# FFN weights split one unit ahead, a fourth seven-product pair, two low halves by accumulating transfer, and the position table moved to layer 0

## The chip, the cores and the metric

The kernel runs on one core of one Trainium2 chip. The metric is the device time of one execution in microseconds. Three runs of the kernel before gave a median of 2230.79 us (2229.18 to 2231.19).

## What is computed

A two-layer encoder trunk on 256 frames of width 2048, in float32. Layer 0 mixes the frames by retention and a gated window unit, layer 1 by a gated linear recurrence and a sparse attention with a relative position bias; after either mixer stands a SwiGLU feed-forward network (FFN) of inner width 5632. Cut to what matters here:

```python
def swiglu(h, wg, wu, wd):
    return (jax.nn.silu(h @ wg) * (h @ wu)) @ wd

for layer in range(2):
    h = rms_norm(x, ln_mix_g[layer])
    x = x + (even_mixer(h, ...) if layer == 0 else odd_mixer(h, ..., rel_bias))
    h = rms_norm(x, ln_ffn_g[layer])
    x = x + swiglu(h, w_ffn_gate[layer], w_ffn_up[layer], w_ffn_down[layer])

# in odd_mixer, the relative bias of the attention's logits
bias = rel_bias[rel_bucket(idx - t[None, :, None])]
```

## The kernel before, in words

Every weight is read from HBM once, as float32, and multiplied in three products of 128x512 tiles: weight and activation are each cut into a high part that TensorE takes exactly (`hi`) and a rest (`lo`), and high times high, high times low and low times high are accumulated in PSUM.

**Loading and splitting.** `load` (L92) brings one 1 MB tile, called a unit here, into one of three `raw` buffers over SP's queue. `piece` (L99) splits half a unit: ACT copies it into `hi` (L103), DVE subtracts into `lo` (L104); there are four `hi` and four `lo` buffers, so two units are split at most. A `raw` buffer is free again when its last reader on ACT or DVE is done, and SP, which issues in order, then starts the third load after it.

**Gate and up.** `gate_up` (L282) makes 512 columns of both gate and up. It is called eleven times in each layer, in parts of four, four and three; behind each part come the `down` products of that part (four column blocks, `gemm`, L125). A call takes eight units, each a pair of 128-row slices of gate and up, which hold a 2x2 block of weights. Five units go by eight products each, of three matmuls, so 24 matmuls. Three units, `MIXED = (1, 4, 6)` (L31), go by a Winograd form of seven products, so 21 matmuls: it needs four sums of the weight blocks (`sum`, L317 to L319, on DVE), and splits three weight blocks (`hu`, `lu`) and the four sums (`ht`, `lt`; L324, L325). `sum`, `hu`, `lu`, `ht` and `lt` have one buffer each. The products collect in eight PSUM banks, `q1` to `q8`, of which 1, 5, 6, 7 belong to the four banks of tag `sm`, and 2, 3, 4, 8 to the four of tag `mm`.

**End of a group.** When the last seven-product unit is done, ACT copies `q1` and DVE makes `u2`, `u3`, `v`, `w` (L338 to L343); when the eighth unit is done DVE adds the other banks (L350), and ACT and DVE do the gate (L353, L354). The result is put on a list, `late`, and transposed by PE into two `sm` banks (`pt_hid`, L188) when the next call has done its first unit; ACT and DVE split the transposes into `hid` (L194, L195).

**Order.** The program is written unit by unit: load, split, multiply. A scheduler lays the instructions of each engine in one queue, and each engine takes its queue in order.

**The position table.** Before layer 1's mixer, POOL loads `onehot` and `rel_bias`, PE multiplies them (`pbias`, L555), ACT copies the result to `bt` (L557), and POOL writes it 128 times into a table in HBM (`skew`, 1536 KB, L558), from which layer 1 reads its bias (L843). The first matmuls of layer 1's mixer, `pz` (L581), of 360 columns, read eight units `od_z` of 720 KB.

Of the kernel before, what the change touches and what calls it, by code (L numbers as in the profile page):

```python
# [10 lines left out]
F32 = mybir.dt.float32  # L11
# [3 lines left out]
OP = mybir.AluOpType  # L15
# [11 lines left out]
RAW = 3  # L27
WARM = 7
TB = 17
TF = 10  # L30
MIXED = (1, 4, 6)  # L31
# [5 lines left out]
def trunk(ctx: ExitStack, tc: tile.TileContext, d: dict, out: bass.AP):  # L37
# [4 lines left out]
    wp = ctx.enter_context(tc.tile_pool(name="weights", bufs=4))  # L42
# [56 lines left out]
    def piece(raw, o, k, n):  # L99
        e = k * n  # L100
        hi = wp.tile([128, 1024], F32R, tag="hi", name="hi")
        lo = wp.tile([128, 1024], F32R, tag="lo", name="lo")
        nc.scalar.copy(hi[:, :e], raw[:, o : o + e])  # L103
        nc.vector.tensor_sub(lo[:, :e], raw[:, o : o + e], hi[:, :e].bitcast(F32))  # L104
        return (hi[:, :e].rearrange("p (k n) -> p k n", n=n), lo[:, :e].rearrange("p (k n) -> p k n", n=n))

# [175 lines left out]
    def gate_up(w, n, fp):  # L282
# [3 lines left out]
        q = {}  # L286

        def bank(i):
            if i not in q:
                q[i] = (PS if i in (1, 5, 6, 7) else PM)([512], f"q{i}")  # L290
                return q[i], True
            return q[i], False

        def product(i, x2, hi, lo, last=False):
            (xh, xl), (ps, first) = x2, bank(i)
# [4 lines left out]
        c = {}  # L300
        for j in range(8):
            raw = load(w[j], 2048)
            end = j == 7
            if j not in MIXED:
                a = n.tiles[j]
                for o, cols in ((0, ((2, 0), (4, 1))), (1024, ((3, 0), (8, 1)))):
                    hi, lo = piece(raw, o, 2, 512)
                    for i, th in cols:
                        t = slice(128 * th, 128 * th + 128)
                        for e in range(2):  # L310
                            kt = 1 - e if o else e
                            product(i, (a[:, kt, 0, t], a[:, kt, 1, t]), hi[:, e, :], lo[:, e, :], end and e == 1)
            else:
                a11, a12, a22, d1, d2, d3, d4 = n.tiles[j]
                r = raw.rearrange("p (i n) -> p i n", i=4)
                sm = fp.tile([128, 4, 512], F32, tag="sum", name="sum")
                nc.vector.tensor_add(sm[:, 0:2, :], r[:, 0:3:2, :], r[:, 3:4, :].to_broadcast([128, 2, 512]))  # L317
                nc.vector.tensor_add(sm[:, 2, :], sm[:, 0, :], r[:, 2, :])
                nc.vector.tensor_add(sm[:, 3, :], sm[:, 2, :], r[:, 1, :])  # L319
                parts = []  # L320
                for src, m, name in ((r[:, 0:3, :], 3, "u"), (sm, 4, "t")):
                    hi = fp.tile([128, m, 512], F32R, tag="h" + name, name="h" + name)
                    lo = fp.tile([128, m, 512], F32R, tag="l" + name, name="l" + name)
                    nc.scalar.copy(hi, src)  # L324
                    nc.vector.tensor_sub(lo, src, hi.bitcast(F32))  # L325
                    parts += [(hi[:, i, :], lo[:, i, :]) for i in range(m)]
                b11, b21, b22, s1, s2, s3, s4 = parts
                last = j == MIXED[-1]
                product(1, a11, *b11, last)
                product(2, a12, *b21)  # L330
                product(3, d3, *b22)
                product(5, d1, *s1, last)
                product(7, d4, *s2, last)
                product(6, d2, *s3, last)
                product(4, a22, *s4)
                if last:
                    c1 = T([512], "c1")
                    nc.scalar.copy(c1, q[1])  # L338
# [652 lines left out]
```

## Time and profile before

| | |
|---|---|
| median of three runs | 2230.79 us (2229.18 to 2231.19) |
| profiled execution: its own time | 2230.81 us |
| profiled execution: span | 2229.0 us |
| busy PE, DVE, ACT, POOL | 2211.7, 1613.1, 1107.1, 12.1 us |
| weights read from HBM | 414.29 MB, 188 GB/s over the span |
| FFN of layer 0, FFN of layer 1 (from the transposes) | about 387 to 1097, 1518 to 2225 us |

The profile is one execution seen by the hardware profiler. A matmul's length in it is the time through the array and overlaps the next one's; how fast PE goes is read from the distance between starts. PE's share of busy time is therefore no measure of its pace.

### The profile page before, as it was taken

What the parts mean: (1) busy time and instruction counts of PE and PEld (TensorE: products, weight loads), DVE (VectorE), ACT (ScalarE), POOL (GpSimd) and SP (SyncE); (2) the same over time, 40 slices, a digit from 0 to 9 for tenths busy, and PEclk for the clock granted to TensorE, in tenths of its full rate; (3) what the DMA queues carried; (4) which work ended last, traced back from release to release, by engine and by line L of the source; (5) the groups of instructions that cost most, each with busy time, mean ns of one, the idle gap of its engine ahead of it and who ended that gap; (6) DMA issues with size and microseconds to landing.
All of it is one profiled execution on the core that took longest, in us unless ns stands there. A gap on an engine that the chain in (4) does not pass through costs nothing.

```text
span 2229.0 us, 26164 instructions
## 1 busy us (share of the span) xinstructions
PE 2211.7 (99%) x10199; PEld 1833.3 (82%) x10199; DVE 1613.1 (72%) x2161; ACT 1107.1 (50%) x1302; POOL 12.1 (1%) x24
## 2 busy tenths in 40 slices
PE   9999999999999999999989999999999999999999
PEld 7888888888888888888878888888888888888887
DVE  6745667988578965886535788869885688857974
ACT  6444436655445543554445355546554455434543
POOL 0000000000000000000000000000000000000000
PEclk9999999999999999999999999999999999999999
DMA  8555444554565455555555343355554555456544
GB/s 328 203 192 190 156 167 177 219 208 170 189 217 203 184 186 192 208 205 183 152 192 198 128 154 130 120 188 208 200 200 168 213 198 195 182 192 225 190 170 151
DMA packets 63435, 419.65 MB, mean 188 GB/s; under 512 B 7672, under 2 KB 7672, under 8 KB 15696
## 3 DMA queue, kind: packets, MB, share of 16 engines
q1 hardware_dynamic: 60704, 412.51, 51.0%
q0 software_dynamic: 1312, 3.33, 0.8%
q10 hardware_dynamic: 1296, 2.15, 0.3%
q8 instruction: 80, 1.31, 0.2%
q14 instruction: 43, 0.35, 0.0%
HBM read 414.29 MB, written 3.67 MB: 188 GB/s over the span
## 4 chain that ended last, share of the span: by engine, by line
PE 97%; DMA 1%; DVE 1%; ACT 0%; issue 0%; SPq 0%; ACTq 0%
PE q L296 14%; PE q L297 14%; PE q L298 14%; PE pd L149 7%; PE pd L148 7%; PE pd L147 7%; PE po L149 3%; PE po L148 2%; PE po L147 2%; PE pqk L149 1%; PE pqk L148 1%; PE pqk L147 1%; PE plv L758 1%; DMA raw<-in_od_z 1%; PE pt_hid L188 1%; PE pvs L147 1%
## 5 line engine op out<-in xcount | busy, mean ns | idle before, releaser
L103 ACT CAST hi<-raw 128x1024 fp32r<-128x1024 f32 (+3 forms) x652 | 677.6, 1040 | 936.1 <-PE q L298 277.4
L104 DVE TENSOR_TENSOR lo<-raw,hi 128x1024 fp32r<-128x1024 f32 (+3 forms) x652 | 781.8, 1206 | 492.1 <-ACT hi L103 490.6
L297 PE MATMUL q<-lo,A 128*128 128x512 f32 x880 | 343.1, 390 | 0.0
L296 PE MATMUL q<-hi,A 128*128 128x512 f32 x880 | 343.1, 390 | 0.0
L298 PE MATMUL q<-hi,A 128*128 128x512 f32 x880 | 342.6, 389 | 0.0
L147 PE MATMUL pd<-hi,hid 128*128 128x512 f32 x704 | 274.7, 390 | 0.0
L149 PE MATMUL pd<-hi,hid 128*128 128x512 f32 x704 | 274.0, 389 | 0.0
L148 PE MATMUL pd<-lo,hid 128*128 128x512 f32 x704 | 273.9, 389 | 0.0
L296 PEld LDWEIGHTS q<-hi,A 128*128 128x128 f32 x880 | 165.2, 188 | 35.3
L297 PEld LDWEIGHTS q<-lo,A 128*128 128x128 f32 x880 | 165.2, 188 | 35.3
L298 PEld LDWEIGHTS q<-hi,A 128*128 128x128 f32 x880 | 165.2, 188 | 35.0
L325 DVE TENSOR_TENSOR lt<-sum,ht 128x2048 fp32r<-128x2048 f32 x66 | 151.0, 2287 | 44.9 <-ACT ht L324 44.9
L324 ACT CAST ht<-sum 128x2048 fp32r<-128x2048 f32 x66 | 126.2, 1912 | 59.8 <-PE q L298 51.9
L149 PEld LDWEIGHTS pd<-hi,hid 128*128 128x128 f32 x704 | 132.1, 188 | 27.4
L148 PEld LDWEIGHTS pd<-lo,hid 128*128 128x128 f32 x704 | 132.2, 188 | 27.3
L147 PEld LDWEIGHTS pd<-hi,hid 128*128 128x128 f32 x704 | 132.2, 188 | 27.1
L325 DVE TENSOR_TENSOR lu<-raw,hu 128x1536 fp32r<-128x1536 f32 x66 | 115.7, 1753 | 14.6 <-ACT hu L324 14.6
L324 ACT CAST hu<-raw 128x1536 fp32r<-128x1536 f32 x66 | 97.6, 1479 | 49.6 <-PE q L298 32.9
L297 PE MATMUL q<-lt,A 128*128 128x512 f32 x264 | 104.5, 396 | 0.0
L298 PE MATMUL q<-ht,A 128*128 128x512 f32 x264 | 104.3, 395 | 0.0
L296 PE MATMUL q<-ht,A 128*128 128x512 f32 x264 | 103.6, 395 | 0.0
L317 DVE TENSOR_TENSOR sum<-raw 128x1024 f32<-128x1024 f32 x66 | 80.3, 1217 | 0.0
(385 smaller groups left out, 3411.0 us busy)
## 6 DMA issues: line engine op xcount, KB each, us to landing
raw<-in_wgu SPq DMA_DIRECT2D x176, 1024.0 KB, 4.8
raw<-in_wd SPq DMA_DIRECT2D x88, 1024.0 KB, 4.8
raw<-in_ev_in SPq DMA_DIRECT2D x44, 1024.0 KB, 4.8
raw<-in_od_in SPq DMA_DIRECT2D x32, 1024.0 KB, 4.8
raw<-in_ev_out SPq DMA_DIRECT2D x16, 1024.0 KB, 4.9
raw<-in_od_out SPq DMA_DIRECT2D x16, 1024.0 KB, 4.7
raw<-in_od_z SPq DMA_DIRECT2D x8, 720.0 KB, 4.3
raw<-in_ev_in SPq DMA_DIRECT2D x6, 512.0 KB, 7.2
```

Source lines behind the costliest of these rows:

```text
L103: nc.scalar.copy(hi[:, :e], raw[:, o : o + e])
L104: nc.vector.tensor_sub(lo[:, :e], raw[:, o : o + e], hi[:, :e].bitcast(F32))
L147: mm(ps[th], xh[:, c], hi[:, j, :], start=i + j == 0, stop=False)
L148: mm(ps[th], xh[:, c], lo[:, j, :], start=False, stop=False)
L149: mm(ps[th], xl[:, c], hi[:, j, :], start=False, stop=i + j == total - 1)
L188: nc.tensor.transpose(pt[:, j, 128 * th : 128 * th + 128], srcs[th][:, 128 * j : 128 * j + 128], ident)
L296: mm(ps, xh, hi, start=first, stop=False)
L297: mm(ps, xh, lo, start=False, stop=False)
L298: mm(ps, xl, hi, start=False, stop=last)
L317: nc.vector.tensor_add(sm[:, 0:2, :], r[:, 0:3:2, :], r[:, 3:4, :].to_broadcast([128, 2, 512]))
L324: nc.scalar.copy(hi, src)
L325: nc.vector.tensor_sub(lo, src, hi.bitcast(F32))
```

## The change

Nothing is computed otherwise than in float32 by the same three products, but six things are done differently.

1. `KINDS = "sasrsasr"` names how each of the eight units of a gate/up call is made: `s` by seven products, `r` by eight with both parts made as before, `a` by eight with the low part made by a transfer. There are four `s`, two `a` and two `r` units, where there were three seven-product units and five others.
2. For an `a` unit ACT writes `hi` and, by a second instruction, minus `hi` into `al`; POOL then issues a transfer that reads the same half unit from HBM again (512 KB) and adds it onto `al`. DVE has no part in it. The two halves rotate through three buffers.
3. The four sums of an `s` unit are split in two pieces through the common `hi` and `lo` buffers; its products are taken in the order 5, 7, 6, 4, 1, 2, 3, with the sums first and the plain blocks (`hu`, `lu`) last.
4. The units of a whole FFN, `down` included, form one list. Ahead of the use of unit i the loads and splits of unit i+1 (`s`, `r`) and i+3 (`a`) are written into the program.
5. The transposes of a group's result come behind the next call's eighth unit, not its first. In the first call of a layer the units go in the order `FIRST`.
6. `onehot`, `pbias`, `bt` and the write of `skew` stand in layer 0, ahead of its output projection, not ahead of layer 1's mixer. (`val` of layer 1 moves to a buffer of tag `A`.)

```diff
+HI = 4
+ACC = 3
-MIXED = (1, 4, 6)
+KINDS = "sasrsasr"
+AHEAD = {"s": 1, "r": 1, "a": 3}
+FIRST = (1, 0, 3, 2, 5, 4, 6, 7)
+MIXED = tuple(i for i, c in enumerate(KINDS) if c == "s")
...
+    def piece_acc(raw, src, o, fp):
+        hi = fp.tile([128, 1024], F32R, tag="ah", name="ah", bufs=ACC)
+        lo = fp.tile([128, 1024], F32R, tag="al", name="al", bufs=ACC)
+        nc.scalar.copy(hi, raw[:, o : o + 1024])
+        nc.scalar.activation(lo, hi.bitcast(F32), AF.Copy, scale=-1.0)
+        nc.gpsimd.dma_start(lo, src[:, o : o + 1024], accum_op=OP.add)
...
+    def whole(src, kind, fp):
+        raw = load(src, 2048)
+        out = []
+        for o in (0, 1024):
+            hi, lo = piece_acc(raw, src, o, fp) if kind == "a" else piece(raw, o, 2, 512)
+            out += [(hi[:, i, :], lo[:, i, :]) for i in range(2)]
+        return out
...
+    def sums(src, fp):
+        raw = load(src, 2048)
+        r = raw.rearrange("p (i n) -> p i n", i=4)
+        sm = fp.tile([128, 4, 512], F32, tag="sum", name="sum")
+        nc.vector.tensor_add(sm[:, 0:2, :], r[:, 0:3:2, :], r[:, 3:4, :].to_broadcast([128, 2, 512]))
+        nc.vector.tensor_add(sm[:, 2, :], sm[:, 0, :], r[:, 2, :])
+        nc.vector.tensor_add(sm[:, 3, :], sm[:, 2, :], r[:, 1, :])
+        parts = []
+        for i in range(2):
+            hi, lo = piece(sm.rearrange("p i n -> p (i n)"), 1024 * i, 2, 512)
+            parts += [(hi[:, e, :], lo[:, e, :]) for e in range(2)]
+        hu = fp.tile([128, 3, 512], F32R, tag="hu", name="hu")
+        lu = fp.tile([128, 3, 512], F32R, tag="lu", name="lu")
+        nc.scalar.copy(hu, r[:, 0:3, :])
+        nc.vector.tensor_sub(lu, r[:, 0:3, :], hu.bitcast(F32))
...
-            if j == 0:
-                flush()
+            if i == (0 if self.first else 7):
+                flush()
...
+        units = []
         for g0, gn in ((0, 4), (4, 4), (8, 3)):
             hid = []
             for g in range(g0, g0 + gn):
-                late.append(partial(to_mix2, gate_up(wgu[g], n, fp), "hid", hid))
+                gu = GateUp(n, hid, g == 0)
+                units += [(wgu[g, j], KINDS[j], partial(gu.use, i)) for i, j in enumerate(gu.order)]
             for c in range(4):
-                ps = two(512, "pd")
-                gemm(ps, wd[c], pairs(hid), 512, range(g0, g0 + gn))
...
+                dn = Down(c, hid, gn, done if g0 == 8 else lambda c: None)
+                units += [(wd[c, g0 + i], "r", partial(dn.use, i)) for i in range(gn)]
+        ready = {}
+        for i, (_, _, use) in enumerate(units):
+            for k in range(i, min(i + 4, len(units))):
+                src, kind, _ = units[k]
+                if k not in ready and k - i <= AHEAD[kind]:
+                    ready[k] = sums(src, fp) if kind == "s" else whole(src, kind, fp)
+            use(ready[i])
+            ready[i] = None
...
+    onehot = T([384], "onehot")
+    nc.gpsimd.dma_start(onehot[0:32], d["onehot"])
...
     nc.scalar.copy(bt[0:8], ps[0:8])
     nc.gpsimd.dma_start(skew, bt[0:8, None, :].to_broadcast([8, 128, 384]))
+
+    out_proj(d["ev_out"], ((mixa, (2, 3)), (mixb, (0, 1))), nf0)
```

How the queues change is seen at two places. The first is DVE's queue at the end of a gate/up group. Before, with the lows of the seventh unit (`lu`, then `lt`) around the adds that end the group:

```order
L325 TENSOR_TENSOR lu<-raw,hu 128x1536
L340 TENSOR_TENSOR u_3601<-c_3599,q_3420 128x512
L341 TENSOR_TENSOR u_3602<-u_3601,q_3416 128x512
L342 TENSOR_TENSOR v<-q_3412,u_3601 128x512
L343 TENSOR_TENSOR w<-q_3412,u_3602 128x512
L350 TENSOR_TENSOR c_3599<-q_3340,c_3599 128x512
L350 TENSOR_TENSOR u_3602<-q_3347,u_3602 128x512
L350 TENSOR_TENSOR v<-q_3358,v 128x512
L325 TENSOR_TENSOR lt<-sum,ht 128x2048
```

With the change, between the sixth and the seventh call of a layer; the first two rows still belong to the old call (the eighth unit's `lo`, the seventh unit's `lu`), the sums, their two `lo` and the second `lu` to the next call's first unit:

```order
L109 TENSOR_TENSOR lo<-raw,hi 128x1024 x2
L320 TENSOR_TENSOR lu<-raw,hu 128x1536
L310 TENSOR_TENSOR sum<-raw 128x1024
L311 TENSOR_TENSOR sum<-sum,raw 128x512
L312 TENSOR_TENSOR sum<-sum,raw 128x512
L109 TENSOR_TENSOR lo<-sum,hi 128x1024
L372 TENSOR_TENSOR u_5579<-c_5578,q_5324 128x512
L109 TENSOR_TENSOR lo<-sum,hi 128x1024
L373 TENSOR_TENSOR u_5580<-u_5579,q_5320 128x512
L374 TENSOR_TENSOR v<-q_5316,u_5579 128x512
L375 TENSOR_TENSOR w<-q_5316,u_5580 128x512
L320 TENSOR_TENSOR lu<-raw,hu 128x1536
```

Behind these stand one add of a bank (L381), the two `hid` splits (L218), three more adds, the gate (L384) and the sums of the next call's third unit. So the whole preparation of a seven-product unit now stands ahead of the adds of a group's end.

The second place is ACT's queue in layer 0, where the last retention block ends and the output projection begins. Before:

```order
L103 CAST hi<-raw 128x1024 x8
L483 COPY qkT<-pqkT 128x512 x2
L508 ACTIVATE junk,rss<-pav 128x256 x4
L103 CAST hi<-raw 128x1024 x2
L194 CAST mixb<-pt_mixb 128x2x256
```

With the change:

```order
L108 CAST hi<-raw 128x1024 x8
L607 COPY bt<-pbias 8x384
L549 COPY qkT<-pqkT 128x512 x2
L574 ACTIVATE junk,rss<-pav 128x256 x4
L108 CAST hi<-raw 128x1024 x2
```

`bt` is copied there behind the splits of the projection's first units, and POOL's write of `skew` is issued behind it.

## Rows read from the trace of the kernel before

**Rows 1.** The page, part 1: busy us (share of the span) and instructions.

```profile
PE 2211.7 (99%) x10199; PEld 1833.3 (82%) x10199; DVE 1613.1 (72%) x2161; ACT 1107.1 (50%) x1302; POOL 12.1 (1%) x24
```

**Rows 2.** Engines by stretch: us, busy (count) by engine, PEclk, DMA share, GB/s.

```profile
473.97:516.81 42.84, 42.84 (x193) 35.17 (x192) 38.19 (x38) 23.21 (x21) 0.00 (x0) 1.00 0.54 197
...
560.00:689.00 129.00, 129.00 (x571) 106.47 (x570) 86.19 (x81) 60.01 (x55) 0.00 (x0) 1.00 0.56 202
1097.00:1180.00 83.00, 74.31 (x373) 65.81 (x373) 41.62 (x79) 37.67 (x64) 1.10 (x1) 0.94 0.55 166
```

**Rows 3.** PE's matmuls in order of time, 1117 to 1135 us: start, length.

```profile
1118.14 0.33 PE L148 MATMUL pz<-lo,A 128*128 128x360 f32 x1
1118.31 0.32 PE L149 MATMUL pz<-hi,A 128*128 128x360 f32 x1
1126.56 0.67 PE L147 MATMUL pz<-hi,A 128*128 128x360 f32 x1 [7.92 <-ACT hi L103]
...
1134.98 0.33 PE L149 MATMUL pz<-hi,A 128*128 128x360 f32 x1
```

**Rows 4.** DMA issues, 1098 to 1134 us: engine, count, KB, median us to landing.

```profile
raw<-in_od_z SPq DMA_DIRECT2D x4, 720.0 KB, 22.0
skew<-bt POOLq DMA_DIRECT2D x1, 1536.0 KB, 34.8
```

**Rows 5.** PE's matmuls in order of time: first one of each weight pair.

```profile
485.04 0.39 PE L296 MATMUL q<-hi,A 128*128 128x512 f32 x1
...
490.48 0.40 PE L296 MATMUL q<-hu,A 128*128 128x512 f32 x1
...
495.38 0.39 PE L296 MATMUL q<-hi,A 128*128 128x512 f32 x1
...
500.84 0.40 PE L296 MATMUL q<-hu,A 128*128 128x512 f32 x1
...
505.74 0.39 PE L296 MATMUL q<-hi,A 128*128 128x512 f32 x1
```

**Rows 6.** The chain of waits, 425 to 480 us: the hidden transposes.

```profile
431.12 0.87 PE pt_hid L188 x8
...
473.97 0.87 PE pt_hid L188 x8
```

**Rows 7.** DVE's groups by form, 387 to 517 us: busy us, mean ns.

```profile
L104 DVE TENSOR_TENSOR lo<-raw,hi 128x1024 fp32r<-128x1024 f32 x32 | 38.4, 1216 | 2.3 <-ACT hi L103 2.1
L325 DVE TENSOR_TENSOR lt<-sum,ht 128x2048 fp32r<-128x2048 f32 x10 | 22.8, 2284 | 3.8 <-ACT ht L324 3.8
L325 DVE TENSOR_TENSOR lu<-raw,hu 128x1536 fp32r<-128x1536 f32 x9 | 15.8, 1750 | 1.4 <-ACT hu L324 1.4
L317 DVE TENSOR_TENSOR sum<-raw 128x1024 f32<-128x1024 f32 x9 | 10.9, 1215 | 0.0
...
L195 DVE TENSOR_TENSOR hid<-pt_hid,hid 128x512 fp32r<-128x512 f32 x4 | 2.6, 686 | 0.5 <-ACT hid L194 0.5
...
L340 DVE TENSOR_TENSOR u<-c,q 128x512 f32<-128x512 f32 x3 | 2.0, 679 | 0.0
```

**Rows 8.** ACT's groups by form, 387 to 517 us: busy us, mean ns.

```profile
L103 ACT CAST hi<-raw 128x1024 fp32r<-128x1024 f32 x31 | 32.6, 1053 | 40.3 <-PE q L298 34.4 <-DMA raw<-in_wgu 4.9 <-ACT hi L103 0.8
L324 ACT CAST ht<-sum 128x2048 fp32r<-128x2048 f32 x10 | 19.1, 1912 | 8.5 <-PE q L298 5.7 <-DVE sum L319 2.8
L324 ACT CAST hu<-raw 128x1536 fp32r<-128x1536 f32 x9 | 13.3, 1477 | 5.0 <-PE q L298 3.9 <-ACT hid L194 0.9
```

**Rows 9.** Engines by stretch, matmuls into `po` alone: us, PE, PEld, DVE, PEclk, DMA, GB/s.

```profile
287.00:307.00 20.00, 13.71 (x56) 9.95 (x55) 1.35 (x2) 1.00 0.34 113
```

**Rows 10.** DMA over one gate/up group, 473.97 to 516.81 us: queue's share, landing.

```profile
q1 hardware_dynamic: 1152, 8.39, 53.3%
...
raw<-in_wgu SPq DMA_DIRECT2D x8, 1024.0 KB, 4.8
```

**Rows 11.** DMA issues of the whole span, one further row.

```profile
masks<-in_masks POOLq DMA_DIRECT2D x1, 448.0 KB, 3.3
```

More of the change, by code (lines that the diff above doesn't have):

```diff
@@ L41, in trunk @@
     cpool = ctx.enter_context(tc.tile_pool(name="consts", bufs=1))
-    wp = ctx.enter_context(tc.tile_pool(name="weights", bufs=4))
+    wp = ctx.enter_context(tc.tile_pool(name="weights", bufs=HI))
     act = ctx.enter_context(tc.tile_pool(name="acts", bufs=8))
@@ L280, in out_proj, with __init__, product @@
                     late.append(partial(norm.feed, c))
[L282 to L295, printed above, removed]
+    def sums(src, fp):
[13 more added lines that the diff above has]
+        nc.vector.tensor_sub(lu, r[:, 0:3, :], hu.bitcast(F32))
+        parts += [(hu[:, i, :], lu[:, i, :]) for i in range(3)]
+        return parts
+    class GateUp:
+        def __init__(self, n, hid, first):
+            self.n, self.q, self.hid, self.first = n, {}, hid, first
+            self.order = FIRST if first else range(8)
+        def product(self, i, x2, hi, lo, last=False):
+            first = i not in self.q
+            if first:
+                self.q[i] = (PS if i in (1, 5, 6, 7) else PM)([512], f"q{i}")
+            (xh, xl), ps = x2, self.q[i]
             mm(ps, xh, hi, start=first, stop=False)
@@ L298, in product, with use @@
             mm(ps, xl, hi, start=False, stop=last)
[L300 to L308, printed above, removed]
+        def use(self, i, w):
+            j, end = self.order[i], i == 7
+            if KINDS[j] != "s":
+                a = self.n.tiles[j]
+                for e, kt, cols in ((0, 0, ((2, 0), (4, 1))), (1, 1, ((2, 0), (4, 1))), (3, 0, ((3, 0), (8, 1))), (2, 1, ((3, 0), (8, 1)))):
+                    for b, th in cols:
@@ L361, in ffn, with done @@
         fp = f.enter_context(tc.tile_pool(name=f"sums{layer}", bufs=1))
+        def done(c):
+            if norm is None:
+                for th in range(2):
+                    nc.scalar.dma_start(out[:, th, 512 * c : 512 * c + 512], x[c][:, th, :])
+            else:
+                late.append(partial(norm.feed, c))
+        units = []
         for g0, gn in ((0, 4), (4, 4), (8, 3)):
```

124 lines of the change are left out of this document (63 added, 61 removed).

## The prediction, made before the result was known

> **What bounds the kernel now.** I read the busy times first: PE is busy for 2211.7 of 2229.0 us, DVE for 1613.1 [rows 1]. A busy PE can still be a waiting one, so next come the stretches [rows 2]. In a gate/up group and in the down products PE has no idle time and full clock; in the window around the start of layer 1 it is busy for only 74.31 of 83 us, and the clock was granted at 0.94 of full. That is the one large hole. In the gate/up group DVE is busy for 38.19 of 42.84 us, so it has 4.7 us to spare; in the down products it is busy for two thirds of the time.
>
> The hole: one matmul starts at 1118.31 us and the next at 1126.56, which waited 7.92 us for ACT's `hi` [rows 3]. ACT waited for weights: the four `od_z` loads of that window took 22.0 us from issue to landing while POOL's `skew` write, 34.8 us long, was under way [rows 4]. From 1118.31 to 1134.98 there are 27 steps between matmuls; at 0.17 us (1118.14 to 1118.31) they need 4.6 us, and took 16.67. The hole costs **12.1 us**, of which the matmuls at half pace after the wait (the lower clock of rows 2) are a part.
>
> Elsewhere the pace of PE is the bound, and I take it from starts [rows 5]. An eight-product unit takes 5.44 us (485.04 to 490.48), or 5.46 behind a seven-product one (495.38 to 500.84); a seven-product unit takes 4.90 (490.48 to 495.38, again to 505.74). Three of 4.90, three of 5.46 and two of 5.44, with 0.87 of transposes, make 42.8; the group's measured period is 42.85 (431.12 to 473.97) [rows 6]. So PE does nothing but multiply there.
>
> **The change, part by part.**
>
> *A fourth seven-product unit.* It saves only 0.52 us, not three of 24 matmuls, since these matmuls step more slowly (4.90/21 = 0.233 against 5.44/24 = 0.227) and the next unit begins slower: four of 4.90 and four of 5.46 with 0.87 are 42.31, against 42.83. Twenty-two groups: **-11.4 us**, if nothing waits.
>
> *DVE's and ACT's load.* Before, ten `lo` of 1.216 and three times (1.215 + two of 0.68 + 1.750 + 2.284) are 32.0 us a group; after, four `lo` and four times (1.215 + 2 x 0.68 + 1.750 + 2 x 1.216) are 31.9, the adds of 128x512 priced by `u` [rows 7]. DVE's load stays the same: the accumulating transfer pays for the fourth unit. ACT had ten of 1.053 and three of 1.912 + 1.477, together 20.7; it gets 27.0 with twelve copies of 1.053 for `r` and `a` units (the negation priced as the copy that is nearest to it) and four times 2 x 1.053 + 1.477 [rows 8]. With 23.21 of 42.84 us busy before [rows 2] it becomes 29.5: neither fills its engine.
>
> *The position table.* Its write no longer meets the 720 KB loads, so the hole goes: **-12.1 us**. It now meets the output projection of layer 0. There a unit lasts 5.44 us, as it also has 24 matmuls of 512 columns, and of the 20 us from 287 on 6.3 go to other products than the projection's [rows 9]. So in 34.8 us PE uses (34.8 - 6.3)/5.44 = 5.2 units. In the old place a unit lasts 24 x 0.17 = 4.1 us, so PE wanted 8.5 units in 34.8 us; a wait of 7.92 us means that it had 1.9 too few, 6.6. Four of these were the loads that landed [rows 4], so 2.6 were in stock. Four loads of 720 KB are 2.8 units of 1 MB; 2.6 + 2.8 = 5.4 against 5.2, a margin of a fifth of a unit: **+1 us**, with 0 and the old 12.1 as ends. `pbias` and `bt` keep their cost; `bt` stands behind eight splits that PE has not used up.
>
> *Where the change adds a wait.* Unit i's `raw` buffer serves three loads later. By the program's order of loads (seventh, eighth, next call's second, next call's first) the first unit of a call takes the buffer of the seventh unit of the call before. That one is free when its `lu` is written, and `hu` and `lu` have one buffer, free at the end of the fifth unit. So, from a call's start: fifth unit ends at 3 x 4.90 + 2 x 5.46 = 25.6; `hu` on ACT 1.48 and `lu` on DVE 1.75 [rows 7, 8] give 28.9, or 29.9 where `lu` stands behind both `lo` of the eighth unit, as in the queue shown; the load lands 4.8 us later [rows 10], at 33.7 to 34.7. DVE must then do three sums (2.6), two `lo` (2.4), `u2`, `u3`, `v`, `w` (2.7), `lu` (1.75), one bank's add (0.68) and the first `hid` split (0.69): 10.8 us by lengths, 10.3 as these overlap a little (38.19 us busy where the lengths of rows 7 make 40.3). That is 44.0 to 45.0. The bank it frees is wanted by the third product of the next call, at 42.31 + 6 x 0.233 = 43.7. PE is late by 0.3 to 1.3; I take 0.8. The same delay reaches the third unit's first `lo`, so it is not paid twice. It applies where a call follows a call that itself follows one, with transposes pending, and the queue has this order: three times a layer, six in all, **+4.8 us**. In the other ten boundaries either no transposes are pending or the queue has `lu` earlier; the same walk leaves PE 0.2 to 0.5 us of margin. In the first call of a layer two seven-product units stand side by side and `lu` comes 0.4 us late: +0.8 for both layers, and with it 5.6.
>
> *The accumulating transfers.* There are 88, of 512 KB. No row shows such a transfer. From below, a plain POOL load of 448 KB lands in 3.3 us [rows 11]; from above, `skew` with 34.8 us for 1536 KB gives 11.6 for 512. An `a` unit is prepared three units ahead; by the walk its transfers are issued 10 us or more before PE needs them. I take 5 us, near the load, since both ends of it are whole rows in all 128 partitions, where `skew` is written from 8; so nothing at 5, and at 11.6, since four of them make 46.4 us where a group has 42.3, 4.1 us a group or 90 in all. DMA's share in a group was 53.3% for 8.39 MB [rows 10]; 2.1 MB more make 67%.
>
> The Trainium skill says (DMA: Bandwidth & Descriptors, Rules for kernel authors) that an accumulating transfer reads its destination and writes it later. No run here shows it; by that rule the 2.1 MB count about twice, an estimate of 80% from the same row, which leaves the sum as it is but makes the second rival likelier.
>
> **Sum.** 2230.8 (the profiled execution's own time; the median is the same to 0.1) - 11.4 - 12.1 + 1 + 5.6 = 2213.9; I say **2214**.
>
> **The rivals.**
>
> *No waits at all.* The lengths of rows overstate DVE's work, and a `raw` load could land at 4.7. Then the sum is 2230.8 - 11.4 - 12.1 = 2207. For it: DVE's spare 4.7 us a group. Against: the walk has margins of tenths.
>
> *The transfers slow the weight loads; slower than before.* An `a` unit's transfers for the next call are issued just behind its neighbour's `hu`, at about 31 us, when the load for the next call's first unit is in flight. Eight loads fill 53.3% of 42.84 us, 2.85 us each; a transfer of half the bytes would fill the engines for 1.43 us by its bytes and for 11.6 at `skew`'s pace. I take twice the former, 2.85 us, and if it goes first that load lands 2.85 later. Sixteen boundaries then cost up to 2.85 us more each, less the margin of about 0.4 in ten: 2214 + 41 = 2255. It decides against the change from 17/16, about 1.1 us later landing. For it: the `od_z` loads that took 22.0 us beside a POOL transfer [rows 4]. Against: the transfer starts after the load in the walk, and 33% of the engines' time stays free. The Trainium skill has the rule under which this would happen (same page, Queues, rings and completion order): each DMA engine takes packets from the queues in turn.
>
> *The hole only moves.* `skew` starves the projection as it starved `pz`, 12.1 us again: 2214 - 1 + 12 = 2225. For it: the margin above is a fifth of a unit. Against: each unit there lasts 1.4 times as long.
>
> **How the numbers follow.** A measurement of this kernel tells a difference of about 0.2% (4.5 us) from none. Forecast 0.45 (2214), no waits 0.27 (2207), the transfers 0.19 (2255), the hole moves 0.09 (2225, faster by a little or the same). Faster by over 0.2%: 0.45 + 0.27 and a quarter of 0.09, 0.74; within 0.2%: 0.07; slower: 0.19. The range runs from 2204, under the no-wait sum by what a pace nearer 0.227 would add, to 2246, which takes in the moved hole and half of the third case.
>
> **What would show it.** Right: no PE wait at `pz`; loads of `od_z` back near 4 us; gate/up groups at 42.3 to 43.6 us between transposes; DVE idle for some 4 us a group ahead of the first sum, on DMA `raw`; transfers of `al` landing in about 5 us. Wrong: groups over 44 us, landing of `raw` over 6 us, PE waiting for `al`, or a PE wait in the output projection of layer 0 near 310 to 330 us.

## The result and the profile after

The changed kernel takes 2286.53 us (median of 4, 2284.41 to 2289.23); the kernel before, on the same chip, 2230.89. The ratio is 1.0252, 95% interval 1.0234 to 1.0269: slower by 56 us, where 2214 was forecast.

The page of the kernel after, part 1 (busy us, share of the span, instructions):

```profile
PE 2226.1 (97%) x10133; PEld 1821.6 (80%) x10133; DVE 1615.3 (71%) x2235; ACT 1220.6 (53%) x1482; POOL 88.2 (4%) x112
```

PE is busy 14.4 us longer with 66 fewer matmuls, and DVE about as long as before (1615.3 against 1613.1) [rows 1]. So the busy times do not show where the 56 us are; starts do. The table below goes by PE's starts in the profiled executions: a stage lasts from its first matmul to the first of the next, and an FFN ends with the start of its last matmul.

| stage, us | before | after | change |
|---|---|---|---|
| layer 0 up to its projection | 282.3 | 282.7 | +0.3 |
| projection to FFN | 97.5 | 104.7 | +7.2 |
| FFN of layer 0 | 714.4 | 749.2 | +34.8 |
| between the layers | 1.1 | 0.2 | -0.8 |
| layer 1's mixer, `pz` to FFN | 415.2 | 402.9 | -12.3 |
| FFN of layer 1 | 711.6 | 738.9 | +27.4 |

These add to +56.6, the difference of the two spans (2285.6 and 2229.0). All of what the FFNs lose is in gate/up; the `down` parts are the same within 0.1 us (87.95 before and 88.05 after, for four column blocks of four units). Within gate/up, the first four calls of a layer lose 22.2 and 17.6 us, the next four 10.0 and 7.4, the last three 2.3 and 2.0.

Four stretches of the kernel after (us, then busy us and count of PE, PEld, DVE, ACT, POOL, then PEclk, DMA share, GB/s):

```profile
326.00:331.00 5.00, 1.76 (x5) 0.83 (x4) 1.71 (x2) 2.49 (x3) 0.00 (x0) 0.77 0.51 214
331.00:338.00 7.00, 7.00 (x23) 5.49 (x23) 5.36 (x6) 2.55 (x3) 0.00 (x0) 0.68 0.68 246
486.60:537.90 51.30, 46.59 (x192) 36.41 (x190) 38.68 (x42) 28.36 (x30) 3.48 (x4) 0.93 0.68 209
1139.00:1156.00 17.00, 17.00 (x108) 16.90 (x107) 12.41 (x29) 9.14 (x15) 0.00 (x0) 1.00 0.48 152
```

The first two rows are the projection of layer 0: PE is busy for 1.76 of 5 us, and then its clock is granted at 0.68 of full. That is the hole of [rows 2, 3], smaller, in its new place. The last row is the start of layer 1's mixer, where that hole was: PE busy all 17 us, full clock. The third row is the third call of gate/up in layer 0: 51.3 us, with PE busy 46.59, at a clock of 0.93. DVE is busy for no more than 38.68 of them, ACT 28.36, so no engine bounds this group; and the DMA engines, at 0.68, have room on average.

DMA of the whole span (queue: packets, MB, share of 16 engines; then issues: count, KB each, median us to landing):

```profile
q1 hardware_dynamic: 60704, 412.51, 49.2%
q0 software_dynamic: 13984, 49.47, 12.0%
...
raw<-in_wgu SPq DMA_DIRECT2D x176, 1024.0 KB, 7.3
...
al<-in_wgu POOLq DMA_DIRECT2D x88, 512.0 KB, 10.7
...
raw<-in_od_z SPq DMA_DIRECT2D x8, 720.0 KB, 4.3
...
skew<-bt POOLq DMA_DIRECT2D x1, 1536.0 KB, 35.4
```

Three readings. `al` lands 10.7 us after its issue, where the prediction took 5 and set 11.6 as the far end. A load of gate and up weights takes 7.3 us where it took 4.8 [rows 10], and `od_z` is back at 4.3 from 22.0 [rows 4]. And the engines' time of one accumulating transfer can be worked out: POOL's queue `q0` holds them for 12.0% of 2285.6 us, 274 us, of which 18 were there before (0.8% of 2229.0); 256 us by 88 is 2.9 us each. SP's loads hold them for 49.2%, 1125 us for 412.51 MB, so 2.9 us for 1 MB. An accumulating transfer of half a unit costs the engines as much as the load of a whole one.

The chain of waits through that slow call (start, us, what):

```profile
486.97 6.56 DMA raw<-in_wgu
...
498.84 9.64 DMA raw<-in_wgu
...
508.57 1.49 ACT hu L319
...
510.07 1.76 DVE lu L320
511.83 0.60 DVE sum L311
512.44 1.15 DVE lo L109
...
513.63 0.79 PE q L339
514.42 0.43 PE q L340
```

It reads downward: a load that takes 6.56 us, then one of 9.64; when that one lands, `hu`, `lu`, a sum and a `lo` of a seven-product unit are made one behind the other, and PE's matmul waits for that `lo`. The matmuls after it step by 0.43 us in place of 0.23: the trace has the clock at half (1.2 of 2.4 GHz) from 513.0 to 519.8 us, so the wait has cost the clock too. POOL's own rows there show what the 9.64 us load met (start, us, queue's operation, wait before it):

```profile
497.24 0.86 POOL L118 DMA_DIRECT2D al<-in_wgu  x1 [18.72 <-ACT al L117]
500.21 0.86 POOL L118 DMA_DIRECT2D al<-in_wgu  x1 [2.11 <-ACT al L117]
```

One transfer was issued 1.6 us ahead of the load, one 1.4 us behind it; two more weight loads were issued in that time too, 1.3 and 5.9 us behind it. The DMA engines in the 9.65 us of that load (columns as above):

```profile
498.84:508.49 9.65, 8.93 (x39) 7.17 (x40) 4.76 (x5) 4.01 (x4) 0.86 (x1) 1.00 0.97 264
```

In the kernel that leaves the transfers out, the load at the same place of the call is issued at 487.55 us, also with two more loads 1.3 and 5.9 us behind it. The 9.65 us from there:

```profile
487.55:497.20 9.65, 9.65 (x44) 7.88 (x43) 8.17 (x8) 6.45 (x6) 0.00 (x0) 1.00 0.85 315
```

That load landed in 4.7 us. The loads come bunched, so the engines are at 0.85 here even without transfers; with them they are at 0.97 and move fewer bytes (264 GB/s against 315). The mean of 0.68 over the group hid a stretch in which the engines were full.

### The profile page after: what moved, and what is told of

Its sections match the earlier page's. It is cut to its first block, busy times and chain, and to the rows that moved or that the text cites. A ratio compares the mean times of both kernels' runs of the same rounds, so it can differ in the third digit from the quotient of the medians.

```text
span 2285.6 us, 26352 instructions
## 1 busy us (share of the span) xinstructions
PE 2226.1 (97%) x10133; PEld 1821.6 (80%) x10133; DVE 1615.3 (71%) x2235; ACT 1220.6 (53%) x1482; POOL 88.2 (4%) x112
## 3 DMA queue, kind: packets, MB, share of 16 engines
q1 hardware_dynamic: 60704, 412.51, 49.2%
## 4 chain that ended last, share of the span: by engine, by line
PE 48%; DVE 13%; DMA 12%; issue 6%; ACT 4%; POOL 0%; ACTq 0%; DVEq 0%; POOLq 0%; SPq 0%
DMA raw<-in_wgu 10%; PE pd L405 6%; PE pd L406 6%; PE pd L404 6%; PE q L339 4%; DVE lo L109 4%; PE q L340 4%; PE q L338 4%; DVE lu L320 2%; DVE sum L310 2%; DMA al<-in_wgu 2%; ACT hi L108 2%; PE po L171 1%; PE po L172 1%; PE po L170 1%
## 5 line engine op out<-in xcount | busy, mean ns | idle before, releaser
L109 DVE TENSOR_TENSOR lo<-raw,hi 128x1024 fp32r<-128x1024 f32 (+3 forms) x520 | 620.9, 1203 | 439.6 <-ACT hi L108 438.3
L108 ACT CAST hi<-raw 128x1024 fp32r<-128x1024 f32 (+3 forms) x520 | 534.1, 1035 | 598.3 <-PE pd L406 196.2
L339 PE MATMUL q<-lo,A 128*128 128x512 f32 x704 | 279.3, 397 | 21.9 <-DVE lo L109 21.9
L338 PE MATMUL q<-hi,A 128*128 128x512 f32 x704 | 276.3, 399 | 11.2 <-DVE u L381 5.2
L108 ACT CAST hi<-sum 128x1024 fp32r<-128x1024 f32 x176 | 183.3, 1047 | 188.4 <-DVE sum L310 122.4
L340 PE MATMUL q<-hi,A 128*128 128x512 f32 x704 | 275.6, 392 | 0.0
L109 DVE TENSOR_TENSOR lo<-sum,hi 128x1024 fp32r<-128x1024 f32 x176 | 213.8, 1221 | 42.4 <-ACT hi L108 41.7
L320 DVE TENSOR_TENSOR lu<-raw,hu 128x1536 fp32r<-128x1536 f32 x88 | 154.5, 1756 | 30.9 <-ACT hu L319 30.2
L338 PEld LDWEIGHTS q<-hi,A 128*128 128x128 f32 x704 | 131.5, 189 | 51.6 <-ACT hi L108 11.5
L340 PEld LDWEIGHTS q<-hi,A 128*128 128x128 f32 x704 | 133.0, 189 | 27.8
L339 PE MATMUL q<-al,A 128*128 128x512 f32 x352 | 141.2, 401 | 13.5 <-DMA al<-in_wgu 13.5
L406 PEld LDWEIGHTS pd<-hi,hid 128*128 128x128 f32 x704 | 132.2, 188 | 27.4
L340 PE MATMUL q<-ah,A 128*128 128x512 f32 x352 | 140.6, 399 | 0.0
L338 PE MATMUL q<-ah,A 128*128 128x512 f32 x352 | 139.4, 398 | 0.6 <-ACT ah L116 0.6
## 6 DMA issues: line engine op xcount, KB each, us to landing
al<-in_wgu POOLq DMA_DIRECT2D x88, 512.0 KB, 10.7
```

Source lines behind the costliest of these rows:

```text
L320: nc.vector.tensor_sub(lu, r[:, 0:3, :], hu.bitcast(F32))
L338: mm(ps, xh, hi, start=first, stop=False)
L339: mm(ps, xh, lo, start=False, stop=False)
L340: mm(ps, xl, hi, start=False, stop=last)
L406: mm(self.ps[th], xl[:, t], hi, start=False, stop=end and j == 3)
```

## The experiments

Two theories stood at the start. **T**: the accumulating transfers slow the weight loads, and PE waits for them and for `al`. **O**: the new order of preparation, with one buffer each for `sum`, `hu` and `lu`, is late by itself.

### Without the transfers, and with plain ones

```diff
-        nc.gpsimd.dma_start(lo, src[:, o : o + 1024], accum_op=OP.add)
```

> Leaves out the 88 accumulating transfers: `al` stays at minus `hi`, so the low part of the a units is not computed. Theory T (the transfers slow the weight loads, and PE waits for `al`): the two FFN stages lose the 62.2 us that they gained and come to the forecast's 5.8 us under before, so about 2218 us, with loads of wgu landing near 4.8 us again instead of 7.3. Rival O (the new order of preparation is late by itself, whatever the transfers do): hardly any change, over 2265 us, calls 2 and 7 of a layer still at 48 to 50 us.

Measured: 2223.86 us, ratio 0.9973 (0.9962 to 0.9984). The loads and the queue are as before:

```profile
q0 software_dynamic: 1312, 3.33, 0.9%
...
raw<-in_wgu SPq DMA_DIRECT2D x176, 1024.0 KB, 4.8
```

T holds, O falls as the cause of the loss: calls 2 and 7 of layer 0 (counted from 0) take 41.5 us, where they took 50.2 and 49.4. The two FFN stages together take 1425.9 us, 62.2 less than after, and 0.1 less than before. So the transfers are the whole loss of the FFNs. But the forecast's other half falls too: even for nothing, they would have bought 0.1 us, not 5.8. (More on that below.)

```diff
-        nc.gpsimd.dma_start(lo, src[:, o : o + 1024], accum_op=OP.add)
+        nc.gpsimd.dma_start(lo, src[:, o : o + 1024].bitcast(F32R))
```

> The same 88 transfers of 512 KB, at the same places, but they overwrite `al` instead of adding to it (so the low part of the a units is wrong in value). Ta (the adding costs: it has to read what it adds to): `al` lands in 3.5 to 5 us and not 10.7, a transfer takes half of its share of the DMA engines, and the time falls below 2235 us. Tb (the bytes and the second queue are what crowds the loads): `al` still lands in 8 us or more, and the time stays over 2270 us.

Measured: 2249.78 us, ratio 1.0087 (1.0071 to 1.0102).

```profile
q0 software_dynamic: 13984, 49.47, 7.4%
...
raw<-in_wgu SPq DMA_DIRECT2D x176, 1024.0 KB, 6.4
...
al<-in_wgu POOLq DMA_DIRECT2D x88, 512.0 KB, 8.8
```

Neither Ta nor Tb alone: the FFNs lie 26.2 us over those without transfers and 36.0 under those of the change. A plain transfer of 512 KB holds the engines for (7.4% of 2249.0, less 18)/88 = 1.7 us, against 2.9. Still its landing only falls from 10.7 to 8.8: most of that time is there without the adding.

### The table alone, put back, and written otherwise

table_back has the block from `onehot` to the write of `skew` in its old place, in the change; table_alone has it in its new place, in the kernel before.

> The change with the position table stored where it was before, ahead of layer 1's mixer. If the stages add up: the 7.2 us in the output projection of layer 0 go, the 12 to 13 us at the start of layer 1 come back, 2286.5 + 5 = 2292 us. If the table has a part in what the FFN of layer 0 loses (34.8 us against 27.4 in layer 1): under 2286 us, with the first four groups of layer 0 nearer to those of layer 1.

Measured: 2293.36 us, ratio 1.0281 (1.0267 to 1.0295). The stages add up: `pz` to FFN is 416.1 us again, the projection 97.5. The FFN of layer 0 still takes 745.7, so 31.3 of its 34.8 us are there without the table; the other 3.5 are no more than the executions of the change differ by (2284.4 to 2289.2).

> Before, with nothing but the position table moved to layer 0. If the hole moves in part, as the trace of the change shows: -12.5 + 7 us, about 2225 us. If the projection's stall there comes from the rest of the change: about 2219 us. If the loads of the old projection have less ahead and the hole moves whole: 2230 us.

Measured: 2222.52 us, ratio 0.9967 (0.9955 to 0.998). The hole moved in part: the projection stage takes 101.4 us, 3.8 more than before, the mixer of layer 1 11.9 less. Over the kernels with the same code up to there (three `raw` buffers, the table written from 8 partitions in layer 0) this stage took 101.4 to 104.9 us. With four `raw` buffers, below, it takes 98.3 in spite of the slow write. The forecast of +1 put it on a margin of a fifth of a unit; it is over the edge by 4 to 7 us. In the kernel after, the write is under way from 292.56 to 327.93 us. The three projection loads issued in the middle of it, at 307 to 318 us, land only when it ends or later:

```profile
raw<-in_ev_out SPq DMA_DIRECT2D x3, 1024.0 KB, 17.8
```

```diff
+    rb = T([8, 16], "rb")
+    nc.vector.tensor_copy(rb[0:32], relb[0:32, :, None].to_broadcast([32, 8, 16]))
-    mm(ps[0:8, :], relb[0:32, :], onehot[0:32, :], start=True, stop=True)
+    mm(ps, rb[0:32].rearrange("p h s -> p (h s)"), onehot[0:32, :], start=True, stop=True)
...
-    nc.scalar.copy(bt[0:8], ps[0:8])
-    nc.gpsimd.dma_start(skew, bt[0:8, None, :].to_broadcast([8, 128, 384]))
+    nc.scalar.copy(bt, ps)
+    nc.gpsimd.dma_start(skew.rearrange("h (s r) n -> (h s) r n", r=8), bt[:, None, :].to_broadcast([128, 8, 384]))
```

> Before with the table moved to layer 0, and written from 128 partitions (each table row made 16 times by the matmul, and written 8 times) and not from 8. If the 34 us of the write come from its 8 partitions: it lands in about 11 us (448 KB of `masks` took 3.3), the 3.8 us that the projection loses with the table in layer 0 go, 2218 to 2219 us. If they come from the number of rows written: it still takes over 25 us and the time is 2222 us.

Measured: 2218.74 us, ratio 0.9947 (0.9934 to 0.9959), the projection stage at 98.4.

```profile
skew<-bt POOLq DMA_DIRECT2D x1, 1536.0 KB, 9.2
```

The same 1536 KB land in 9.2 us from 128 partitions, in place of 34.8 [rows 4]. This kernel has none of the change but the table, and is 12 us under before.

### The first call of a layer

```diff
-FIRST = (1, 0, 3, 2, 5, 4, 6, 7)
+FIRST = (3, 0, 1, 2, 5, 4, 6, 7)
```

PE's rows in the first call of the change (start, us, operation, wait before it) show why it was tried: an `a` unit comes first there, and its `al` has no time to land.

```profile
393.78 0.51 PE L339 MATMUL q<-lo,A 128*128 128x512 f32 x1 [0.44 <-DVE lo L109]
400.18 0.80 PE L339 MATMUL q<-al,A 128*128 128x512 f32 x1 [5.89 <-DMA al<-in_wgu]
```

> The change with the first call of a layer in the order r, s, a, s, a, s, s, r (FIRST begins 3, 0, 1, 2) in place of a, s, r, s, a, s, s, r. If the 10 to 11 us that the first call of each layer loses are its wait for the first `al` (6.4 us, and the slower clock behind it), both first calls fall to 43 or 44 us and the time to about 2268 us. If another thing is late there (the first weights, the norm), they stay at 50 us or more and the time over 2282 us.

Measured: 2290.59 us, ratio 1.0264 (1.0248 to 1.028). A miss: the first calls fall from 51.7 and 52.7 us to 49.0 and 47.7, but the second ones rise from 43.8 and 43.2 to 49.7 and 49.9. What is taken away in one call turns up in the next.

That only 0.1 us of the gain is left without transfers has its place at the first and second call too. There the other calls run at their pace (41.2 to 41.5 us from first to last matmul, but for one of 41.9; periods of 42.2 to 42.5 where one of 42.85 was measured before [rows 6]). Only the first two of each layer lose: 2.1 and 2.8 us in layer 0, 1.1 and 4.2 in layer 1, in steps that waited. The change's `FIRST` sets two seven-product units side by side there, as sixth and seventh. So, in the kernel without the transfers:

```diff
-FIRST = (1, 0, 3, 2, 5, 4, 6, 7)
+FIRST = (1, 0, 2, 3, 4, 5, 6, 7)
```

> The kernel without the transfers (the low part of the a units is not computed) with FIRST = (1, 0, 2, 3, 4, 5, 6, 7), so that the two seven-product units that stand side by side in the first call of a layer are its second and third, not its sixth and seventh. If that pair at the end of the first call makes the second call late (2.8 and 4.2 us above a step there), the second calls fall to about 41.5 us, the first parts of gate/up from 174.6 and 174.8 to about 170, and the time to 2213 to 2216 us. If the loss only moves to the first call: 2221 to 2226 us.

Measured: 2225.44 us, ratio 0.9977 (0.9968 to 0.9987). The rival holds: the second calls lose 1.5 and 1.6 us now, the first ones 4.0 and 3.7. Some 5 us a layer stay, wherever the pair stands. That the pair is their cause is not shown: no order without one was run, and one of the first call's waits without transfers ends, by the trace, with a row of the norm (`nr_y`, 0.7 us), not with weights.

### Other ways to make the low parts

```diff
-KINDS = "sasrsasr"
+KINDS = "srsrsrsr"
```

> The change with KINDS = srsrsrsr: no transfers, DVE makes the low parts of all four other units, four more of 1.22 us a group, which makes 43.1 us of DVE in a group of 42.3. If DVE then bounds the group: periods of 43.1 to 44.5 us, 2229 to 2260 us in all, loads of wgu near 4.8 us. If not (the lengths overlap, or waits elsewhere hide it): 42.3 to 42.6 and 2218 to 2225 us. Either way it stays under the change itself, if the transfers are what costs.

Measured: 2234.75 us, ratio 1.0022 (1.0013 to 1.0031). The first four calls of layer 0 in one stretch (PE, PEld, DVE, ACT, POOL, PEclk, DMA, GB/s):

```profile
387.80:565.00 177.20, 171.52 (x754) 137.19 (x754) 168.37 (x202) 102.55 (x110) 0.00 (x0) 1.00 0.52 185
```

DVE is busy for 168.37 of 177.2 us, which is about what PE needs for four calls where nothing waits (168.4, the second part of gate/up in change_raw4 below). Calls 4, 5, 8 and 9, the first two behind `down` with its lighter load, run at 40.9 to 41.0 us; calls 1, 3 and 7 take 44.6 to 46.0. PE's own waits there are for ACT (10.2 us for `hi`, 5.4 for `hu`), whose copies stand behind a late sum of DVE's or behind the copy of a transpose. That it is DVE's load is shown by two runs below: no_acc_raw4 has calls 3 and 7 of layer 0 at 46.2 us, one_acc_raw4, which makes one unit's low part by transfer (2.4 us a call less for DVE, and more for ACT), at 41.2.

```diff
-        nc.scalar.activation(lo, hi.bitcast(F32), AF.Copy, scale=-1.0)
-        nc.gpsimd.dma_start(lo, src[:, o : o + 1024], accum_op=OP.add)
+        nc.gpsimd.tensor_sub(lo, raw[:, o : o + 1024], hi.bitcast(F32))
```

> The change with the low part of the a units by a subtraction on POOL (GpSimd), in place of ACT's negation and the transfer; the output is the same. No row shows how long POOL takes for 128x1024. If it is under some 5 us and leaves DVE alone: as without the transfers, about 2224 us or, as ACT has less to do, a little under. If POOL and DVE hold each other up: DVE's `lo` longer than 1.22 us and over 2235 us.

Measured: 2343.72 us, ratio 1.0507 (1.0492 to 1.0521). Groups by form (busy us, mean ns, idle before):

```profile
L117 POOL TENSOR_TENSOR al<-raw,ah 128x1024 fp32r<-128x1024 f32 x88 | 263.3, 3006 | 1298.3 <-ACT ah L116 1225.1 <-PE q L338 48.4 <-PE q L339 24.5
L109 DVE TENSOR_TENSOR lo<-sum,hi 128x1024 fp32r<-128x1024 f32 x176 | 246.0, 1404 | 23.9 <-ACT hi L108 23.1
```

POOL takes 3.0 us for what DVE does in 1.2, and DVE's own `lo` of the sums, 1.22 in the kernel after, takes 1.40; PE waits for DVE's `lo` for 57.5 us in all, against 21.9 in the kernel after. The Trainium skill (Perfetto Trace Analysis, Optimizing Scalar/DVE Operations) says that the two engines share a read port, so that moving work between them might not help. These rows agree in that DVE is slower while POOL works; the port itself they do not show.

```diff
-KINDS = "sasrsasr"
+KINDS = "sasrsrsr"
```

> The change with KINDS = sasrsrsr: one a unit a call in place of two, 44 transfers and not 88, and 2.44 us more of DVE a group. If the cost is the number of transfers: half of the 62 us between the change and the kernel without transfers stays, 2255 us. If two transfers in a call can go where no load is pressing and only the next two hurt, under 2240 us, near or under the 2234.75 without any a unit. If one pair of transfers hurts as much as two: over 2270 us.

Measured: 2250.72 us, ratio 1.0089 (1.0073 to 1.0106). Near half: the FFNs lie 27.4 us over those without transfers, against 62.2 with 88. But the half is not spread evenly. The two first calls (51.5 and 51.6 us) lose 17.3 us over those without transfers, with two `a` units 18.5; the other calls lose 10.1, with two `a` units 43.7. So the number of transfers is not the measure of the cost, and the forecast of 2255 came near by luck.

no_acc_mid is no_acc with the table written from 128 partitions and with the transposes behind the fifth unit (`if i == (0 if self.first else 4)`); no_acc_mid_order has the `FIRST` of nt_early_pair besides.

> A try for a faster kernel: the change without transfers (KINDS = srsrsrsr), the table written from 128 partitions, and the transposes of a group behind the fifth unit of the next call, not behind the eighth. Without transfers the third and fourth calls of a part waited 2.6 us, with ACT behind the copy of the transposes. If that wait is the place of the transposes: groups near 42 us, 2213 to 2220 us. If DVE's 43.1 us a group bind: 2228 us or more, as before less the 3.8 us of the table.

> The same with FIRST = (1, 0, 2, 3, 4, 5, 6, 7). If the pair of seven-product units at the end of the first call makes the second late (45.1 and 44.6 us without transfers): 4 to 6 us under the kernel with the transposes in the middle alone. If not: the same within 2 us.

Measured: 2233.78 us, ratio 1.0012 (1.0002 to 1.0021), and 2237.23, ratio 1.003 (1.0019 to 1.0042). Both miss as tries: with the transposes elsewhere calls 3 and 7 still take 45.5 us and more, and the second kernel is 3.5 us slower than the first, which neither case of its forecast has.

### Late loads, or the wait for al?

T has two ways to reach PE. The list of waits of the kernel after (engine and line, what it waited for: us in total, times, longest) names both:

```profile
DVE sum L310 <- DMA raw<-in_wgu: 82.3, 38, 4.5
...
ACT ah L116 <- DMA raw<-in_wgu: 43.9, 22, 4.1
...
ACT hu L319 <- DMA raw<-in_wgu: 25.6, 8, 5.5
...
PE q L339 <- DVE lo L109: 21.9, 23, 2.1
...
PE q L339 <- DMA al<-in_wgu: 13.5, 5, 5.9
```

PE itself waits for `al` only 5 times. But DVE and ACT wait for weights, and PE's waits for DVE's `lo` come behind that. Not all of it is harm: with the new order DVE is often ready ahead of its load, and the kernel without the transfers, in which PE hardly waits, has this row:

```profile
DVE sum L309 <- DMA raw<-in_wgu: 54.4, 27, 4.0
```

ACT's waits for weights ahead of `ah` are 10.9 us there, against 43.9. If late loads are it, a fourth `raw` buffer must help. It has room only with fewer buffers for `ah` and `al`, hence a control.

```diff
-ACC = 3
+ACC = 2
...
-RAW = 3
+RAW = 4
```

> Control for the next: the kernel with one a unit a call (2250.7 us), with two buffers for `ah` and `al` in place of three. One a unit a call needs two at a time, so 2248 to 2253 us; if a free buffer is waited for, some us more.

> The same with four `raw` buffers in place of three, so that each load of a unit is issued a unit earlier. If what remains of the transfers' cost is weight loads that land late (up to 9.6 us in place of 4.8), the second to fourth calls of a layer fall to 41.5 to 42 us and the time by 8 us or more, to 2242 or under; the first call's 10 us, its wait for `al`, stay. If the wait is for `al` or for DVE, four buffers change nothing: within 3 us of the control.

Measured: the control 2251.13 us, ratio 1.0089 (1.0072 to 1.0106); with four `raw` buffers 2225.07, ratio 0.9977 (0.9968 to 0.9987). 26 us go with one buffer. In the profiled executions 18.5 of them are in the FFNs; 6.5 are in the projection of layer 0 (104.9 to 98.3), where it is the table's write that makes loads late. A call of layer 0 then looks so:

```profile
479.10:521.30 42.20, 42.20 (x192) 34.61 (x189) 40.21 (x44) 26.52 (x28) 1.75 (x2) 1.00 0.72 243
```

42.2 us, PE busy throughout at full clock, though the engines' share is 0.72 and `al` still takes 10.0 us to land. Late loads were it, but for the first call of a layer, which keeps 52.6 and 51.7 us.

> The change without transfers (KINDS = srsrsrsr), with the table written from 128 partitions and four `raw` buffers. With three buffers and the table fast it would be 2231 us (2234.75 less 3.8). If a load that is issued too late is behind the 2.6 us waits of the third and fourth call: under 2222 us. If DVE's load or the order of ACT's queue is: 2228 to 2233 us.

Measured: 2230.77 us, ratio 0.9999 (0.999 to 1.0009). The FFNs take 1437.4 us, against 1436.1 in no_acc: without transfers the fourth buffer gives nothing. Loads land in 4.8 us there, and DVE is what the kernel waits for.

> The change itself, two a units a call, with four raw buffers (and two for ah and al, for which the control showed no difference). If late weight loads behind three buffers are what costs, as with one a unit: the calls after the first at 41.3 to 42 us, the first still 10 us over, 2225 to 2235 us. If two a units crowd the DMA engines beyond what a fourth buffer covers: over 2255 us.

Measured: 2230.98 us, ratio 0.9999 (0.999 to 1.0008): the change with `RAW = 4` and `ACC = 2` loses 55.5 us of its 56, some 6 of them in the projection. It is then as fast as before: what the table gains (12.3 us between the stages), the FFNs lose (11.4), in their first calls. All calls after the first but one (44.1 us) run at 41.2 to 41.7; the first calls keep 52.4 and 51.4.

```profile
raw<-in_wgu SPq DMA_DIRECT2D x176, 1024.0 KB, 5.8
...
al<-in_wgu POOLq DMA_DIRECT2D x88, 512.0 KB, 9.8
```

PE's waits in this run answer the question, and so does one of its calls (columns as above):

```profile
PE q L339 <- DMA al<-in_wgu: 11.8, 2, 6.0
...
PE q L339 <- DVE lo L109: 0.9, 2, 0.5
```

```profile
695.34:737.57 42.23, 42.23 (x189) 34.52 (x188) 37.59 (x40) 27.89 (x28) 3.47 (x4) 1.00 0.83 249
```

The waits behind late loads fall from 21.9 us to 0.9; those for `al` stay, two of them, one in the first call of each layer. And the call keeps full pace with the DMA engines at 0.83, more than the 0.68 of the slow call.

### Tries for a faster kernel

one_raw4_r has one `a` unit a call, `RAW = 4`, `ACC = 2`, the table written from 128 partitions and the `FIRST` of first_r; change_raw4_r is the same with two `a` units.

> A try for a kernel faster than both: one a unit a call, four raw buffers, the table written from 128 partitions, and the first call of a layer beginning with an r unit, so that its first al is issued two units earlier. With all other calls at 41.1 us, the first call's 10.4 us a layer are the last large loss. If it is the wait for al alone: first calls at 42 to 43 us, 2205 to 2209 us. If the wait only moves to the second call, as it did with three buffers: 2219 to 2224 us.

Measured: **2215.41 us**, ratio 0.9928 (0.9916 to 0.994), the lowest median of all. The interval touches that of spread_table, which is far simpler. The first calls fall to 47.8 and 47.0 us, not to 42 or 43: though the first `al` is now prepared two units ahead, PE still steps for 4.3 and 3.7 us at it. Every other call takes 41.05 to 41.5.

> The same with two a units a call, as in the change. If the engines have room for 88 transfers: within 3 us of the one with 44 (DVE has 2.4 us less a call, which nothing waits for). If not: 10 us or more over it.

Measured: 2235.12 us, ratio 1.0019 (1.0009 to 1.0028), 20 us over it: the first calls take 57.2 and 54.1 us. Most of the other calls differ by only 0.1 to 0.2 us. So the engines do have room for 88 transfers in the steady calls, and not at a layer's start, where PE waits for both `a` units of the first call (4.3 and 6.0 us in layer 0). A first call without any transfer was not run in this kernel.

## Why the prediction was wrong, step by step

- **The bound and the pace.** Right, in part by luck. PE bounds, and where nothing waits a call's period is 42.23 to 42.35 us, without transfers as well as with two `a` units and four buffers (calls 5 and 6 of layer 0), forecast 42.31, before 42.85. Two terms were off by some 0.3 us a call each and cancel: in change_raw4 a seven-product unit takes 4.82 or 4.84 us (forecast 4.90), an `a` unit 5.60 (forecast 5.46).
- **DVE's load unchanged by the change.** Right: 1615.3 us busy against 1613.1; and no_acc shows that without the transfers it would not have been.
- **The hole at `pz` goes: -12.1.** Right: -12.3 in that stage and -0.8 ahead of it.
- **The table's new place: +1, with 0 and 12.1 as ends.** Mis-sized: +7.2, and 3.8 to 7.3 over kernels with the same code there. The margin of a fifth of a unit was less than the working could bear. It counted four loads of the old place as landed during the write, by their median of 22.0 us; the fourth landed 1.5 us after the write's end (at 1134.97 us, the write at 1133.48). In the new place two units landed in its 35.4 us (at 294.6 and 298.6), where 2.8 were counted: 0.8 of a unit fewer, by estimate 4.4 us of PE's work at 5.44 a unit, where the margin was 1.1. (A unit there lasts 1.3 times as long as at `pz`, 5.44 against 4.1, not 1.4.) With three buffers neither place had room for a write of 35 us; written from 128 partitions it costs 0.9 us in the new one (98.4 against 97.5), and with a fourth buffer the slow write costs no more (98.3).
- **Where the change adds a wait: +5.6.** Too small, and in the wrong places. The walk found it at the seventh, eighth and eleventh call; without transfers those take 41.3 to 41.9 us. The loss lies in the first and second call, 10.2 us for both layers, where 0.8 us had been put. So the forecast for the FFNs was 5.7 us too low even without the transfers' cost: at -0.1 in place of -5.8 the sum would have been some 2220.
- **The accumulating transfers: "I take 5 us, near the load ... so nothing at 5".** This is the step that failed: a term that was put at nothing costs 62.2 us in the FFNs. They land in 10.7 us, next to the far end of 11.6. But the way in which 11.6 was to cost (four transfers one behind the other, longer than a group, up to 90 us) is not what the runs show either, and that 62.2 lies under 90 is luck: the transfers overlap (497.24 to 504.71 and 500.21 to 511.41 us in the call shown), and PE waits for `al` for only 13.5 us, 11.8 of which a fourth buffer leaves. They cost by way of the weight loads, 7.3 us where they took 4.8. The choice of the nearer row rested on shape (whole rows in 128 partitions); plain_transfer shows that even a plain transfer of this kind takes 8.8 us beside these loads. The row of 3.3 us met one weight load; the same transfer of `masks` takes 5.9 us in the kernel after, where it meets two.
- **The rival "the transfers slow the weight loads", 2255, at 0.19.** The right mechanism, with too small a price. Its 2.85 us of engine time a transfer, taken as twice what the bytes need, was right (2.9 measured). What it left out: a load meets more than one transfer (9.64 us in the chain above, 4.8 late and not 2.85), calls in the middle are hit as those at boundaries, the matmuls behind a wait stepped by 0.43 us at the lower clock, and the first call waits for `al` itself. In PE's steps of gate/up, those over 0.6 us make 53.2 us, against 7.1 without transfers, and those of 0.38 to 0.6 us, most of them at half clock, 11.1, against 2.1 (each step counted less 0.229 us, the pace).
- **DMA's share of 67%, or of 80% if the adding counts twice.** The second was near: 0.83 in the call of change_raw4 that ran at full pace, 0.54 in the like call without transfers. The Trainium skill's rule (DMA: Bandwidth & Descriptors, Rules for kernel authors: an accumulating transfer reads its destination and writes it later) agrees with that and with 2.9 us of engine time against 1.7 for a plain one. But the share did not decide: 0.68 in the slow call shown, 0.83 in the quick one. The Trainium skill's section on queues (same page, Queues, rings and completion order: each engine takes packets from its queues in turn) agrees with the loads' 6.4 us beside plain transfers.

## What to carry to other kernels

A transfer that takes work from a busy engine isn't paid for in bytes but in the landing time of the loads beside it: ask how late a load may be before an engine runs dry (here three buffers left next to nothing, and a fourth was worth 18.5 us in the FFNs with one transfer pair a call and 50.7 with two), not how full the DMA engines are on average. When two rows bound an unknown price 3.3 to 11.6, and the sum turns from gain to loss between them, the forecast is the chance of each and not the nearer row. And a slow broadcast write is better made fast at its source (8 partitions to 128: 34.8 to 9.2 us) than moved to another place.

## What the runs showed of the hardware

- An accumulating transfer of 512 KB from HBM onto SBUF holds the DMA engines for 2.9 us, a plain one for 1.7, a 1 MB load for 2.9; landing 10.7, 8.8 and 4.8 us (the load alone).
- Reading 8 partitions 128 times each into HBM took 34.2 to 35.6 us for 1536 KB; 128 partitions 8 times each, 9.1 to 9.3.
- A subtraction of 128x1024 float32 on POOL took 3.0 us, 2.5 times DVE's; with it about, DVE's own of the sums took 1.40 us in place of 1.22.
- With four seven-product units, calls with two, one and no `a` units took 41.21, 41.05 and 40.89 us where nothing waited. An `a` unit takes 5.60 us and an `r` unit at its place 5.46, in no_transfer too, so it is not the transfer; the cause was not tried.
